# Which half's norm comes first: the order of root, diagonal, spread and scalings at the start of the second layer

## The chip, the core and the metric

The kernel runs on one core of one Trainium2 chip. The metric is the device time of one execution in microseconds (us). The kernel before takes 1287.84 us, the median of three runs (1287.13, 1287.84 and 1291.49).

## The reference

A backbone of two layers works on 1024 tokens of width 1024. The first layer (a convolution branch and a recurrent branch, with 256 context tokens) ends in a gated residual. The second layer is the one that matters here:

```python
x = x + gate * out_x                       # end of the first layer
hx = rmsnorm(x, norm_g) * (1 + scale) + shift   # the second norm
u, g = split(hx @ w_in, 2)                 # 2048 columns each
d = windowed_mean(u) - u                   # windows 2, 4, 8, 16 within rows of 64 tokens
y = einsum(d, w_grp) * od_scale            # four groups of 512 x 512
x = x + gate * ((y * silu(g)) @ w_out)
return rmsnorm(x, final_g)
```

All of it is float32. The root of the norm is one number per token: one over the square root of the mean of the squares of its 1024 features.

## The kernel before, in words

**Layout.** Features lie on the partitions, tokens along the free axis: `x1` is eight tiles `x_0` to `x_7` of 128 features by 1024 tokens. The tokens are worked in two halves of 512, called half 0 and half 1 here; `HALF[h]` is the slice of a tile.

**Float32 products.** TensorE multiplies rounded operands, so each operand is split in a high part and a low part (`split`, L101 to L103: a cast on ScalarE, then a subtraction on VectorE or GpSimd). A product is then three matmuls: high by high (L998), high by low (L1000), low by high (L1001). Names that end in h and l are such parts.

**The seven-product scheme.** The large products of the second layer cut both operands in 2 x 2 blocks and form seven block products in place of eight (`quad`, L1009 to L1037). The token operands are b11, t1, t2, b21, t3, b22 and t4, each of four tiles; they are sums and differences of the scaled quarters of `x1`, made in a loop over i (L1354 to L1373). The weights go through `wquad` (L960 to L990), which loads two raw tiles (`wr_`), forms sums (`ws_v` and the like) and splits them (`wq_v`). In `quad`, three PSUM banks are used: qa takes the first product (b11), is copied by ScalarE into bank qb (L1014), qc takes the second (t1), qb the third (t2) on top of the copy, and so on. So the third product can't start before that copy. The products of u (name `v`) and of the gate (name `g`) follow one another in sixteen such groups.

**The fold.** The group weights `w_grp` are multiplied into the columns of `w_in` for u ahead of time, since pooling is linear over tokens (`fold`, L241 to L270). For a group, the raw group weights (`graw`) are loaded and split into gh and gl. Then follow four weight blocks kp: each loads a raw block (`wr_wu`) from SyncE's queue, ScalarE casts it to `wh_wu` (L102), GpSimd makes `wl_wu` (L103), and for two slices s TensorE does twelve matmuls; ScalarE copies the result from PSUM (`fo`, L265) and issues the store to `wfold` in DRAM from its own queue (L266). The tiles of `fo` come from a pool of two, and so do the raw tiles `wr`, which `wquad` uses too. `v_weights` loads the folded weights (`wr_v`) back from `wfold`. Groups 2 and 3 are folded here, between the first layer's last product (`woa`) and the second layer's first one: this is the work that TensorE has while the norm is made.

**The second norm.** While the last products of the first layer come out, `square_acc` adds up the squares of each half in `nacc[h]` (in the profile n1acc). For each half, `rstd_cols` (L196 to L212) does four steps: four matmuls (L202) that sum over the partitions and leave the sums of 512 tokens as four columns; a square root on ScalarE (L203) and a reciprocal on VectorE (L206); a product with the unit matrix on VectorE that makes four diagonal blocks (L208, `dg_n`); and a matmul of ones by these diagonals (L211), which spreads each token's root over all 128 partitions into a PSUM bank (`ms_n`). `scaled` (L1337 to L1340) multiplies a half of a tile by the feature's scale `a` and this spread root: sixteen scalings, 128 by 512 each. Half 1 of the squares is complete first; half 0 gets its last term from the last tile, `x_7`.

**The order.** Each engine works its instructions in one fixed sequence. A scheduler writes it, with its own timeline estimate, from the program order, the dependences and some hints: `high_priority` draws an instruction forward (the copies of `quad` have it, L1013 and following), and `issue_after(x)` keeps the instructions of a block behind x on their engine. In the kernel before, `rstd_cols` is called for half 0 and then for half 1 (L1303); four steps of the two folds are free of it (L1304 and L1305), the rest of the folds stands behind both square roots (L1306 to L1311). In the blocks' loop the scalings of half 0 and half 1 are written by turns.

Of the kernel before, what the change touches and what calls it, by code (L numbers as in the profile page):

```python
# [15 lines left out]
P = 128  # L16
# [39 lines left out]
def body(ctx, tc, xT, ctxT, cc, ccol, modT, modW, win, gw, wout, wu, grp, wg, wo1, small, edge, ident, outT):  # L56
# [136 lines left out]
        nc.vector.reciprocal(acc, rt[:, :n])  # L193


    def rstd_cols(acc, name, idD, rpool, wn, marks=None):  # L196
        n = acc.shape[-1]
        nt = n // P
        ps, root = banks(f"ms_{name}", wn)
        r = rpool.tile([P, H // P], F32, tag=f"rc_{name}", name=f"rc_{name}")[:, :nt]  # L200
        for c in range(nt):
            nc.tensor.matmul(ps[:, c : c + 1], acc[:, c * P : (c + 1) * P], ones[:, 0:1], start=True, stop=True)  # L202
        root_done = nc.scalar.activation(r, ps[:, :nt], AF.Sqrt, bias=eps_r)  # L203
        if marks is not None:
            marks.append(root_done)
        nc.vector.reciprocal(r, r)  # L206
        t = ttile(f"dg_{name}")[:, :n]
        nc.vector.tensor_tensor(out=t.rearrange("p (c t) -> p c t", t=P),  # L208
                                in0=idD.unsqueeze(1).to_broadcast([P, nt, P]),
                                in1=r.unsqueeze(2).to_broadcast([P, nt, P]), op=mult)  # L210
        nc.tensor.matmul(root[:, :n], ones, t, start=True, stop=True)  # L211
        return root[:, :n]  # L212

# [25 lines left out]
    def fold(g, raw_tile, out_tile, g_tile=None, w_tile=None):  # L239
        g_tile = g_tile or dtile  # L240
        gh, gl = [], []  # L241
        for i in range(2):
            raw = raw_tile(f"graw_{g}_{i}")
            load(raw, grp[g, i])
            th = g_tile(f"gh_{g}_{i}", F32R)
            tl = g_tile(f"gl_{g}_{i}", F32R)
            split(raw, th, tl, nc.vector)
            gh += [th[:, 0:H], th[:, H:D]]
            gl += [tl[:, 0:H], tl[:, H:D]]
        yield  # L250
        if w_tile is not None:
            ws = [wload(wu[g, kp], f"wu_{g}_{kp}", nc.gpsimd, out=w_tile[kp]) for kp in range(KT // 2)]
            yield
        for kp in range(KT // 2):
            wh, wl = wload(wu[g, kp], f"wu_{g}_{kp}", nc.gpsimd) if w_tile is None else ws[kp]
            for s in range(2):
                ps = psum(f"fold_{g}_{kp}_{s}")
                for i in range(4):
                    kc = slice(i * 2 * P + s * P, i * 2 * P + (s + 1) * P)
                    nc.tensor.matmul(ps, wh[:, kc], gh[i], start=(i == 0), stop=False)  # L260
                    nc.tensor.matmul(ps, wh[:, kc], gl[i], start=False, stop=False)
                    nc.tensor.matmul(ps, wl[:, kc], gh[i], start=False, stop=(i == 3))
                dst = wfold[g][:, :, 2 * kp : 2 * kp + 2, :]
                o = out_tile(f"fo_{g}_{kp}_{s}")
                nc.scalar.copy(o, ps)  # L265
                nc.scalar.dma_start(dst[:, :, s, :].rearrange("m p c -> p m c"),  # L266
                                    o.rearrange("p (m c) -> p m c", c=P))
            yield
# [1645 lines left out]
```

## Time and profile before

| what | value |
|---|---|
| median of three runs | 1287.84 us (1287.13 to 1291.49) |
| the profiled execution | 1293.0 us |
| its span in the profile | 1291.2 us |
| mean granted clock of TensorE | 0.996 |
| busy: ScalarE, GpSimd | 642.1 us, 353.6 us |
| time of the DMA queues' packets, first queue | 40.3% of 16 engines |
| HBM read and written | 136.72 MB and 44.04 MB |

PE is TensorE's matmuls, PEld its weight loads, DVE is VectorE, ACT ScalarE, POOL GpSimd, SP SyncE; ACTq and SPq are an engine's DMA issues. A row of a timeline gives the start in us from the start of the span, the time in us, the engine, the line of the kernel, the operation, its tiles (out <- in, buffer numbers left out), partitions by elements, and a count where like instructions are drawn together; in square brackets stands the idle time of the engine before it and what ended that. A matmul's row holds its latency: matmuls overlap, so the pitch is the distance of two starts. A table by windows gives, for each stretch, the busy time of PE, PEld, DVE, ACT and POOL in this order (instructions in brackets), then the granted clock (1 is full speed), the busy share of the DMA engines and GB/s.

### The profile page before, as it was taken

The page shows a single profiled execution, that of the slowest core. Times are in us where ns is not written, and L with a number is a line of the kernel's source. Part 1 is how long each engine was busy: PE and PEld are TensorE (multiplying, and loading weights), DVE is VectorE, ACT ScalarE, POOL GpSimd, SP SyncE. Part 2 cuts the span into 40 slices and gives each one's busy share as a digit, 9 for nine tenths or more (in the row PEclk, how much of TensorE's full clock was granted, in tenths as well). Part 3 has the DMA queues.
Part 4 walks back from the last instruction along what each step waited for, and adds up shares of the span by engine and source line. Part 5 has one row for each costly group of instructions (what it writes and reads, how often), then busy time and mean ns, then how long its engine had stood idle before and what let it go on. Part 6 is the DMA issues. An engine that isn't in the chain of part 4 may idle for free.

```text
span 1291.2 us, 15810 instructions
## 1 busy us (share of the span) xinstructions
PE 1272.3 (99%) x5634; PEld 1026.7 (80%) x5634; DVE 1146.3 (89%) x1763; ACT 642.1 (50%) x941; POOL 353.6 (27%) x180
## 2 busy tenths in 40 slices
PE   8999999999999999999999999999999999999997
PEld 4468888888888888888887888788888888878786
DVE  7979999999999989999789758998999987887876
ACT  5343656566657633237435345734434444654543
POOL 3063655675558603543210022000000000000002
PEclk9999999999999999999999999999999999999998
DMA  9934111121212133542555356244233324778723
GB/s 371 355 118 152 58 41 66 41 74 42 66 41 90 55 109 109 182 146 95 171 189 189 129 173 202 83 155 139 93 134 132 123 104 150 246 243 268 285 83 130
DMA packets 82931, 181.80 MB, mean 141 GB/s; under 512 B 7842, under 2 KB 27682, under 8 KB 82852
## 3 DMA queue, kind: packets, MB, share of 16 engines
q1 hardware_dynamic: 74404, 176.60, 40.3%
q10 hardware_dynamic: 8448, 4.20, 1.1%
q8 instruction: 44, 0.72, 0.2%
q14 instruction: 35, 0.29, 0.1%
HBM read 136.72 MB, written 44.04 MB: 140 GB/s over the span
## 4 chain that ended last, share of the span: by engine, by line
PE 82%; DMA 8%; DVE 4%; ACT 2%; issue 2%; POOL 1%; SPq 0%; POOLq 0%; ACTq 0%; DVEq 0%
PE vg L510 7%; PE wob L510 7%; PE va L510 7%; PE gb L510 7%; PE xb L510 6%; PE g L510 4%; PE fold L285 3%; DMA x_part<-xp 2%; PE qb_v L998 2%; PE qb_v L1001 2%; PE qb_v L1000 2%; PE ga L510 2%; PE ga L134 2%; PE ga L133 2%; PE ga L135 2%
## 5 line engine op out<-in xcount | busy, mean ns | idle before, releaser
L510 DVE SCALAR_TENSOR_TENSOR conv<-u,sm,conv 128x505 f32<-128x505 f32 (+6 forms) x224 | 153.7, 744 | 0.9
L1703 POOL TENSOR_TENSOR o<-x,rr 128x256 f32<-128x256 f32 (+1 forms) x10 | 9.4, 970 | 447.6 <-ACT rr L1639 445.7
L510 POOL TENSOR_TENSOR l<-l,l 128x1280 f32<-128x1280 f32 (+1 forms) x23 | 63.9, 2796 | 91.8 <-DVE l L510 65.5
L510 ACT ACTIVATE l<-g,sm 128x512 f32<-128x512 f32 (+1 forms) x96 | 58.7, 619 | 57.8 <-PE g L510 56.0
L285 PE MATMUL fold<-graw,wu 128*128 128x512 f32 x128 | 58.0, 614 | 2.2 <-DMA wu<-wu 2.2
L285 PEld LDWEIGHTS fold<-graw,wu 128*128 128x128 f32 x128 | 25.1, 197 | 33.7 <-issue 32.6
L102 ACT CAST wq_g<-wr_g 128x512 fp32r<-128x512 f32 x48 | 28.3, 621 | 45.6 <-DVE wr_g L979 17.6
L510 PE MATMUL wob<-ybh,wh_wob 128*128 128x512 f32 x128 | 50.6, 396 | 0.0
L510 PE MATMUL gb<-h0h,wl_gb 128*128 128x512 f32 x128 | 49.9, 390 | 0.3 <-POOL wl_gb L510 0.3
L510 PE MATMUL vg<-h0h,wl_vg 128*128 128x512 f32 x128 | 50.0, 390 | 0.0
L510 PE MATMUL gb<-h0h,wh_gb 128*128 128x512 f32 x128 | 49.8, 389 | 0.0
L510 PE MATMUL wob<-ybh,wl_wob 128*128 128x512 f32 x128 | 49.8, 389 | 0.0
L510 PE MATMUL gb<-h0l,wh_gb 128*128 128x512 f32 x128 | 49.8, 389 | 0.0
L510 PE MATMUL vg<-h0h,wh_vg 128*128 128x512 f32 x128 | 49.8, 389 | 0.0
L510 PE MATMUL vg<-h0l,wh_vg 128*128 128x512 f32 x128 | 49.8, 389 | 0.0
L510 PE MATMUL va<-h0h,wh_va 128*128 128x512 f32 x128 | 49.8, 389 | 0.0
L510 PE MATMUL va<-h0l,wh_va 128*128 128x512 f32 x128 | 49.8, 389 | 0.0
L510 PE MATMUL va<-h0h,wl_va 128*128 128x512 f32 x128 | 49.8, 389 | 0.0
L510 PE MATMUL wob<-ybl,wh_wob 128*128 128x512 f32 x128 | 49.8, 389 | 0.0
L510 DVE TENSOR_TENSOR_SCAN l<-l,l 128x256 f32<-128x256 f32 (+1 forms) x32 | 48.7, 1521 | 1.1
L103 POOL TENSOR_TENSOR wl_wu<-wr_wu,wh_wu 128x1024 fp32r<-128x1024 f32 x8 | 19.2, 2402 | 108.7 <-ACT wh_wu L102 108.7
L510 POOL TENSOR_TENSOR l<-l,uc 128x1280 f32<-128x1280 f32 x16 | 48.2, 3033 | 0.0
(618 smaller groups left out, 4342.9 us busy)
## 6 DMA issues: line engine op xcount, KB each, us to landing
mod<-modT SPq DMA_DIRECT2D x20, 512.0 KB, 5.4
x_part<-xp SPq DMA_DIRECT2D x32, 256.0 KB, 3.5
mod<-modT SPq DMA_DIRECT2D x32, 256.0 KB, 3.3
wr_v<-wfold SPq DMA_DIRECT2D x16, 512.0 KB, 3.4
wr_g<-wg SPq DMA_DIRECT2D x16, 512.0 KB, 4.5
wr_wo<-wo SPq DMA_DIRECT2D x16, 512.0 KB, 4.8
y_b<-y SPq DMA_DIRECT2D x24, 256.0 KB, 3.3
y_t<-y SPq DMA_DIRECT2D x24, 256.0 KB, 3.4
```

What stands on the lines that cost most here:

```text
L102: return (nc.scalar.copy(hi, src), eng.tensor_tensor(out=lo, in0=src, in1=hi.bitcast(F32), op=sub))
L103: eng.tensor_tensor(out=lo, in0=src, in1=hi.bitcast(F32), op=sub))
L133: nc.tensor.matmul(ps, hi[:, kc], xh[k][:, cols], start=(k == 0), stop=False)
L134: nc.tensor.matmul(ps, hi[:, kc], xl[k][:, cols], start=False, stop=False)
L135: nc.tensor.matmul(ps, lo[:, kc], xh[k][:, cols], start=False, stop=(k == ks - 1))
L285: nc.tensor.matmul(ps, w[:, kc], gs[i], start=(i == 0), stop=(i == 3))
L510: last[eng] = f(*args, **kw)
L998: nc.tensor.matmul(ps, hi, xh[k], start=(first and k == 0), stop=False, skip_group_check=not first)
L1000: nc.tensor.matmul(ps, hi, xl[k], start=False, stop=False, skip_group_check=not first)
L1001: mm = nc.tensor.matmul(ps, lo, xh[k], start=False, stop=(k == KH - 1), skip_group_check=not first)
L1703: nc.gpsimd.tensor_tensor(out=outs[k // per][:, k % per], in0=x1[k][:, cols], in1=rr, op=mult)
```

## The change

`rstd_cols` gives its last column matmul, its diagonal and its spread matmul back in a list, and is called for half 1 first. All of half 0's steps are kept behind half 1's diagonal on VectorE and behind half 1's spread on TensorE. Two pieces of the fold of group 2 are kept behind half 1's steps on TensorE: its second weight block behind the columns, its third behind the spread. The first step of group 3 (loading and splitting its group weights) is kept behind half 1's square root. In the loop over the blocks, the scalings of half 1 other than those of the first i are kept behind half 0's diagonal on VectorE; before that they may come, while half 0's root is still being made.

```diff
-    def rstd_cols(acc, name, idD, rpool, wn, marks=None):
+    def rstd_cols(acc, name, idD, rpool, wn, marks=None, spread=None):
...
         for c in range(nt):
-            nc.tensor.matmul(ps[:, c : c + 1], acc[:, c * P : (c + 1) * P], ones[:, 0:1], start=True, stop=True)
+            col = nc.tensor.matmul(ps[:, c : c + 1], acc[:, c * P : (c + 1) * P], ones[:, 0:1], start=True, stop=True)
...
-        nc.tensor.matmul(root[:, :n], ones, t, start=True, stop=True)
+        mm = nc.tensor.matmul(root[:, :n], ones, t, start=True, stop=True)
+        if spread is not None:
+            spread += [col, diag, mm]
         return root[:, :n]
+
+    pe_order = {}
...
                 ps = psum(f"fold_{g}_{kp}_{s}")
...
+                with ExitStack() as fctx:
+                    for mm in pe_order.get((g, kp, s), ()):
+                        fctx.enter_context(tc.issue_after(mm.ins))
...
     marks = []
-    rs = [rstd_cols(nacc[h][:, :H], f"n1{h}", idD, hpool, h, marks) for h in range(2)]
-    for f in (fold2, fold2, fold3, fold2):
+    spread = []
+    rs = [rstd_cols(nacc[1][:, :H], "n11", idD, hpool, 1, marks, spread)]
+    with tc.issue_after(spread[1].ins), tc.issue_after(spread[2].ins):
+        rs.insert(0, rstd_cols(nacc[0][:, :H], "n10", idD, hpool, 0, marks, spread))
+    pe_order[2, 1, 0], pe_order[2, 2, 0] = spread[:1], spread[2:3]
+    for f in (fold2, fold2):
         next(f)
+    with tc.issue_after(marks[0].ins):
+        next(fold3)
+    next(fold2)
...
         b11, b21 = x1[i][:, HALF[0]], scaled(0, KH + i)
-        b12, b22 = scaled(1, i), scaled(1, KH + i)
+        with ExitStack() as sctx:
+            if i > 0:
+                sctx.enter_context(tc.issue_after(spread[4].ins))
+            b12, b22 = scaled(1, i), scaled(1, KH + i)
```

The first place is VectorE at the norm. In the names, gl are the low parts of group 3's group weights, rc_n the reciprocals, dg_n the diagonals and ms_n the spread roots. Before, dg_n_6063 and ms_n_1 belong to half 0, dg_n_6074 and ms_n to half 1:

```order
L103 TENSOR_TENSOR gl_0_6116<-graw_0_6113,gh_0_6115 128x1024
L206 RECIPROCAL rc_n_6067<-rc_n_6067 128x4
L1275 TENSOR_TENSOR n1acc_5498<-n1acc_5498,n1q_1_0_6049 128x512
L103 TENSOR_TENSOR gl_1_6122<-graw_1_6119,gh_1_6121 128x1024
L206 RECIPROCAL rc_n_6056<-rc_n_6056 128x4
L208 TENSOR_TENSOR dg_n_6063<-cH,rc_n_6056 128x512
L208 TENSOR_TENSOR dg_n_6074<-cH,rc_n_6067 128x512
L1339 SCALAR_TENSOR_TENSOR x_0_5502<-x_0_5502,a_135,ms_n_1_6055 128x512
L1339 SCALAR_TENSOR_TENSOR x_1_5503<-x_1_5503,a_135,ms_n_1_6055 128x512
```

With the change, dg_n_6062 and ms_n_6054 belong to half 1, and dg_n_6074 to half 0:

```order
L206 RECIPROCAL rc_n_6055<-rc_n_6055 128x4
L208 TENSOR_TENSOR dg_n_6062<-cH,rc_n_6055 128x512
L103 TENSOR_TENSOR gl_0_6116<-graw_0_6113,gh_0_6115 128x1024
L1282 TENSOR_TENSOR n1acc_5498<-n1acc_5498,n1q_1_0_6049 128x512
L103 TENSOR_TENSOR gl_1_6122<-graw_1_6119,gh_1_6121 128x1024
L1353 SCALAR_TENSOR_TENSOR x_0_5502<-x_0_5502,a_135,ms_n_6054 128x512
L1353 SCALAR_TENSOR_TENSOR x_4_5790<-x_4_5790,a_135,ms_n_6054 128x512
L206 RECIPROCAL rc_n_6067<-rc_n_6067 128x4
L208 TENSOR_TENSOR dg_n_6074<-cH,rc_n_6067 128x512
L1353 SCALAR_TENSOR_TENSOR x_1_5503<-x_1_5503,a_135,ms_n_6054 128x512
L1353 SCALAR_TENSOR_TENSOR x_5_5791<-x_5_5791,a_135,ms_n_6054 128x512
```

Half 1's diagonal has moved ahead of both low splits of the fold, and its scalings begin ahead of half 0's reciprocal; before, both diagonals stood behind the splits, with no scaling between.

The second place is ScalarE at the first group of `v`: the high splits of the token operands (x_b22h, x_t2h, x_b21h, with the tile of `x1` that they come from), a copy of the fold (fo), the copy of `quad` from bank qa to bank qb, and the copy of a finished bank (s_v). Before:

```order
L1334 ACTIVATE x_b21h_6409<-x_5_5791,m_134 128x512
L266 DMA wfold_84<-fo_3_1_6402 128x4x128
L1014 COPY qb_v_6569<-qa_v_6567 128x512
L1334 ACTIVATE x_b22h_6426<-x_6_5936,m_134 128x512
L1334 ACTIVATE x_b22h_6426<-x_7_5937,m_134 128x512
L1334 ACTIVATE x_t2h_6414<-x_3_5645,m_134 128x512
L1334 ACTIVATE x_b21h_6410<-x_6_5936,m_134 128x512
L1334 ACTIVATE x_b21h_6410<-x_7_5937,m_134 128x512
L1042 COPY s_v_6595<-qc_v_6568 128x512
```

With the change:

```order
L1348 ACTIVATE x_b22h_6425<-x_5_5791,m_134 128x512
L273 DMA wfold_84<-fo_3_0_6386 128x4x128
L272 COPY fo_3_1_6402<-fold_3_1_6389 128x512
L1348 ACTIVATE x_b22h_6426<-x_6_5936,m_134 128x512
L1348 ACTIVATE x_b22h_6426<-x_7_5937,m_134 128x512
L1348 ACTIVATE x_t2h_6414<-x_3_5645,m_134 128x512
L1348 ACTIVATE x_b21h_6410<-x_6_5936,m_134 128x512
L1348 ACTIVATE x_b21h_6410<-x_7_5937,m_134 128x512
L1021 COPY qb_v_6569<-qa_v_6567 128x512
L273 DMA wfold_84<-fo_3_1_6402 128x4x128
L1049 COPY s_v_6595<-qc_v_6568 128x512
```

The copy from qa to qb stood ahead of five splits and stands behind them now, and one fold copy with its store has moved into the stretch.

The third place is TensorE at the same group, where the second product (qc_v, token operand t1) meets the third (qb_v, token operand t2). Before:

```order
L998 MATMUL qc_v_6568<-x_t1h_6418,wq_v_5_6456 128x512
L998 MATMUL qb_v_6569<-x_t2h_6413,wq_v_6_6459 128x512
L1000 MATMUL qb_v_6569<-x_t2l_6415,wq_v_6_6459 128x512
L1001 MATMUL qb_v_6569<-x_t2h_6413,wq_v_6_6459 128x512
L998 MATMUL qb_v_6569<-x_t2h_6413,wq_v_6_6459 128x512
L1000 MATMUL qb_v_6569<-x_t2l_6415,wq_v_6_6459 128x512
L1000 MATMUL qc_v_6568<-x_t1l_6420,wq_v_5_6456 128x512
L1001 MATMUL qc_v_6568<-x_t1h_6418,wq_v_5_6456 128x512
```

With the change:

```order
L1005 MATMUL qc_v_6568<-x_t1h_6418,wq_v_5_6456 128x512
L1007 MATMUL qc_v_6568<-x_t1l_6420,wq_v_5_6456 128x512
L1008 MATMUL qc_v_6568<-x_t1h_6418,wq_v_5_6456 128x512
L1005 MATMUL qb_v_6569<-x_t2h_6413,wq_v_6_6459 128x512
L1007 MATMUL qb_v_6569<-x_t2l_6415,wq_v_6_6459 128x512
L1008 MATMUL qb_v_6569<-x_t2h_6413,wq_v_6_6459 128x512
L1005 MATMUL qb_v_6569<-x_t2h_6413,wq_v_6_6459 128x512
L1007 MATMUL qb_v_6569<-x_t2l_6415,wq_v_6_6459 128x512
```

The last two matmuls of the second product now stand ahead of the third product, where five matmuls of it stood before them.

More of the change, by code (lines that the diff above doesn't have):

```diff
@@ L257, in fold @@
                 ps = psum(f"fold_{g}_{kp}_{s}")
[L258 to L262, printed above, removed]
+                with ExitStack() as fctx:
+                    for mm in pe_order.get((g, kp, s), ()):
+                        fctx.enter_context(tc.issue_after(mm.ins))
+                    for i in range(4):
+                        kc = slice(i * 2 * P + s * P, i * 2 * P + (s + 1) * P)
+                        nc.tensor.matmul(ps, wh[:, kc], gh[i], start=(i == 0), stop=False)
+                        nc.tensor.matmul(ps, wh[:, kc], gl[i], start=False, stop=False)
+                        nc.tensor.matmul(ps, wl[:, kc], gh[i], start=False, stop=(i == 3))
                 dst = wfold[g][:, :, 2 * kp : 2 * kp + 2, :]
```

6 lines of the change are left out of this document (3 added, 3 removed).

## The prediction

> **What bounds the kernel now.** I read the page first, then the PE waits, then the timelines of the engines backwards from the longest wait. The page's first line:
>
> ```profile
> PE 1272.3 (99%) x5634; PEld 1026.7 (80%) x5634; DVE 1146.3 (89%) x1763; ACT 642.1 (50%) x941; POOL 353.6 (27%) x180
> ```
>
> PE is the bound: a microsecond counts only where PE waits for it. The waits of PE from 700 us to the end, the two largest (total, times, longest):
>
> ```profile
> PE qb_v L998 <- ACT qb_v L1014: 2.1, 1, 2.1
> PE qb_wo L998 <- ACT b_wo L1563: 1.3, 2, 0.7
> ```
>
> The first lies right behind the changed stretch. PE around it, from the timeline:
>
> ```profile
> 816.44 0.39 PE L1001 MATMUL qc_v<-x_t1h,wq_v 128*128 128x512 f32 x1
> 816.66 0.39 PE L998 MATMUL qc_v<-x_t1h,wq_v 128*128 128x512 f32 x1
> 819.19 0.67 PE L998 MATMUL qb_v<-x_t2h,wq_v 128*128 128x512 f32 x1 [2.14 <-ACT qb_v L1014]
> ...
> 822.64 0.45 PE L998 MATMUL qb_v<-x_t2h,wq_v 128*128 128x512 f32 x1
> 822.93 0.39 PE L1000 MATMUL qb_v<-x_t2l,wq_v 128*128 128x512 f32 x1
> ```
>
> and the table by windows (busy times, then the granted clock, DMA share, GB/s):
>
> ```profile
> 815.00:820.00 5.00, 2.86 (x12) 2.06 (x11) 5.00 (x9) 5.00 (x10) 0.09 (x2) 0.94 0.19 54
> 820.00:825.00 5.00, 5.00 (x18) 3.92 (x16) 5.00 (x9) 2.83 (x5) 0.24 (x2) 0.72 0.61 201
> ```
>
> PE stands still for 2.14 us, and then its clock is granted at half: 0.94 and 0.72 over 5 us each are 0.3 + 1.4 = 1.7 us lost in about 3.4 us. So this place costs about 3.8 us. In those two windows DVE is busy for 5.00 of 5.00 us, and in the first ACT too: the wait is for a copy that stands in ACT's queue behind the splitting of operands, and the splits come from DVE. ACT's timeline (ACTq rows are its DMA issues):
>
> ```profile
> 783.61 1.05 ACT L102 CAST wh_wu<-wr_wu 128x1024 fp32r<-128x1024 f32 x1 [1.54 <-DMA wr_wu<-wu]
> 783.62 0.98 ACTq L266 DMA_DIRECT2D wfold<-fo  x2
> 788.35 0.59 ACT L265 COPY fo<-fold 128x512 f32<-128x512 f32 x1 [3.69 <-DMA wfold<-fo]
> ...
> 790.46 1.05 ACT L102 CAST wh_wu<-wr_wu 128x1024 fp32r<-128x1024 f32 x1 [0.44 <-ACT fo L265]
> ...
> 793.23 2.56 ACT L1334 ACTIVATE x_b11h<-x,m 128x512 fp32r<-128x512 f32 x4
> ...
> 809.89 0.72 ACT L1334 ACTIVATE x_t2h<-x,m 128x512 fp32r<-128x512 f32 x1 [0.44 <-DVE x L1361]
> 810.52 0.57 ACT L265 COPY fo<-fold 128x512 f32<-128x512 f32 x1
> ...
> 818.55 0.58 ACT L1014 COPY qb_v<-qa_v 128x512 f32<-128x512 f32 x1
> ...
> 820.92 1.33 ACT L1334 ACTIVATE x_b21h<-x,m 128x512 fp32r<-128x512 f32 x2
> ```
>
> The copy that PE waits for starts at 818.55. From 809.89 on ACT does not wait; at 809.89 it waited for DVE. DVE's timeline:
>
> ```profile
> 777.89 1.23 DVE L103 TENSOR_TENSOR gl<-graw,gh 128x1024 fp32r<-128x1024 f32 x1 [1.46 <-ACT gh L102]
> 779.03 0.17 DVE L206 RECIPROCAL rc_n<-rc_n 128x4 f32<-128x4 f32 x1
> 779.24 1.29 DVE L208 TENSOR_TENSOR dg_n<-cH,rc_n 128x512 f32<-128x512 f32 x2
> 784.00 10.62 DVE L1339 SCALAR_TENSOR_TENSOR x<-x,a,ms_n 128x512 f32<-128x512 f32 x16 [3.48 <-PE ms_n L211]
> 794.54 4.36 DVE L1335 SCALAR_TENSOR_TENSOR x_b11l<-x,m,x_b11h 128x512 fp32r<-128x512 f32 x4
> 798.83 0.68 DVE L103 TENSOR_TENSOR wq_v<-wr_v,wq_v 128x512 fp32r<-128x512 f32 x1
> 799.75 0.69 DVE L978 TENSOR_TENSOR ws_v<-wr_v,wr_v 128x512 f32<-128x512 f32 x1 [0.25 <-DMA wr_v<-wfold]
> ...
> 808.93 1.28 DVE L1361 TENSOR_TENSOR x<-x,x 128x512 f32<-128x512 f32 x2
> ...
> 818.39 0.68 DVE L103 TENSOR_TENSOR x_t1l<-x,x_t1h 128x512 fp32r<-128x512 f32 x1
> ```
>
> The 3.48 us before the 16 scalings is the idle time that the change goes for: the larger part of this stall looks like its child. But at 799.75 DVE waits once more, 0.25 us, for a weight load that has nothing to do with the norm. That load on the chain that ended last, and POOL's last work before it:
>
> ```profile
> 796.39 3.33 DMA wr_v<-wfold
> ```
>
> ```profile
> 791.59 4.78 POOL L103 TENSOR_TENSOR wl_wu<-wr_wu,wh_wu 128x1024 fp32r<-128x1024 f32 x2 [4.44 <-ACT wh_wu L102]
> ```
>
> The load takes the buffer that POOL's second split leaves at 796.37, and lands at 799.72.
>
> **The change part by part.** *Half 1 first.* Its reciprocal and diagonal come before the next fold's low split; DVE is idle there, and ACT's square root falls in a wait for a load. Nothing on the path; if that cover were gone, 0.17 + 0.65 us of DVE. The spread of half 1 on PE moves forward by one fold block; PE's work is the same. What it costs PE, from the timeline:
>
> ```profile
> 784.96 1.02 PE L211 MATMUL ms_n<-dg_n,ones 128*128 128x512 f32 x2
> ```
>
> So all behind it up to its old place, the columns of half 0 and its spread among them, comes under 1.02 us later on PE (I take 0.9), and what follows is at its old time: 0 in the sum.
>
> *The scalings.* DVE in the new order, by the pitch 10.62 / 16 = 0.66 us: the low split ends at 779.12; two scalings of half 1, to 780.45; reciprocal and diagonal of half 0, 0.17 + 0.65, to 781.3; six scalings, 4.0, to 785.2; by then the spread of half 0 has been through PE (its old release, 784.00, and 0.9); eight scalings, 5.3, to 790.5. Before, the 16 ended at 794.6. DVE gains 4.1 us here: the part does what it says.
>
> *What is late next.* Behind the scalings stand the four low splits x_b11l, which need the casts x_b11h on ACT. These stood at 793.23 without having waited for DVE: ahead of them ACT had to cast the fold's last weights, behind fold copies that waited 3.69 us for stores. The change leaves that queue as it is, and puts one store issue and one more fold copy ahead of the casts: they start 1 us later, near 794.3. So DVE, free at 790.5, idles to about 794.9. The first low split takes long anyway:
>
> ```profile
> L1335 DVE SCALAR_TENSOR_TENSOR x_b11l<-x,m,x_b11h x4: 741/742/2372, 794.5 to 798.2; 128x512 fp32r<-128x512 f32 x4
> ```
>
> 2.37 us against 0.74: it ends half a microsecond after POOL's split (796.37), and will again. DVE then arrives at ws_v as before, at 799.5, and waits for the load to 799.75. Its order from there to the second copy of t1 is unchanged, and it is busy all the time. Of the 4.1 us nothing is left at 799.75. Is the load itself earlier? It hangs on POOL, POOL on the cast at 790.46, that on the fold stores issued at 783.62, those on the load before 783.61, and that on the low split at 777.89, which waits for ACT, not for the norm. None of these is moved. I take 0; bounds of 1 us to both sides, for stores and loads that meet in another order.
>
> *The queue on ACT.* This is the term that remains. From x_t2h at 809.89 on, ACT has the same splits as before, but the copy qb_v<-qa_v now stands behind all of them: behind both x_b22h of blocks 6 and 7, x_t2h of block 3 and both x_b21h of blocks 6 and 7, where it stood ahead of these. One fold copy more (0.57, as at 810.52) falls into this stretch, and the copy itself (0.58) leaves it: they cancel. So the copy starts where the x_b21h at 820.92 end, about 822.15 since neighbours overlap by 0.1, instead of 818.55: +3.6 us. Who waits for it: PE's product qb_v, and everything behind it on PE.
>
> *PE ahead of the copy.* Two matmuls of qc_v, the third block's last two, now stand ahead of qb_v. They need x_t1l, which DVE ends at 819.07, so PE does them inside its wait: at its pitch of 0.22 us (816.44 to 816.66), -0.45 us.
>
> *The clock.* After 2.14 us of idling the half clock took 1.7 us. The new idling is 5.7 us with two matmuls in it. I take 1.7 us again, as the row of the same place; the ends are 0 and 3.4, a second stretch of the same length. The Trainium skill, "TensorE: Matmul & The Clock Gate", section "Part 1: The HAM clock gate", says that the clock is set by windows of 3413 ns which run freely and don't start with the kernel's idling; that fits the 3.4 us here, and by it the slow time after a restart depends on where in a window PE starts again. An estimate from that page: 0 to 6.8 us slow, the sum below from +1.4 to +4.8 us.
>
> *Later order.* The next products are interleaved otherwise (qa_g ahead of the third part of qb_v), SP swaps some stores and loads behind that, none is added. PE's later waits are at most 0.7 us each (second row of the waits): 0, ends -0.7 and +0.7.
>
> Sum: 3.6 - 0.45 + 0 + 0 = +3.15 us, taken as +3.1. Against the profiled execution: 1293.0 (span 1291.2 and 1.8 around it) becomes 1296.1. The profiled execution lies 5.2 us over the median of the three runs, 1287.84, which I take as the base: 1290.9.
>
> **The rivals.**
>
> *The gain arrives.* If the load landed 4 us earlier, or ACT passed its splits to DVE earlier, the copy would stand where PE never waits, and both the 2.1 us and the 1.7 us go: 1287.84 - 3.8 = 1284.0. For it: DVE does gain 4.1 us at 790.5. Against: the wait at 799.75 and POOL's row, neither of which the change touches. It decides when the load lands before 796. Chance 0.10.
>
> *A part arrives.* One of the fold's stores goes out earlier than I think, and the load lands 1 to 3 us earlier; each microsecond takes as much off the copy's start. At 2 us: 1288.9. Chance 0.13.
>
> *The clock's second stretch.* The longer idling covers the whole of one stretch of 3.4 us, so PE starts again at half clock and keeps it for a second one: 1.7 us more, +4.8, 1292.6. That is slower by more than the 0.3% (3.9 us) which a measurement of this kernel can tell from no change. For it: 2.1 us of idling already took the clock. Against: the two matmuls in the idling, and that the row shows only one stretch. It decides from an idling that outlasts the stretch after the drop; the Trainium skill's windows, above, allow it. Chance 0.17.
>
> **How the numbers follow.** The forecast has 0.60: predicted 1290.9, its own range 1289.5 to 1292.3 by the load's bound of 1 us and the later order's 0.7. The range of 8 in 10 takes in most of the part that arrives and the second stretch, and leaves out the full gain and the tails: 1287.0 to 1293.2. Faster by over 0.3% (under 1283.98): half of the full gain and little else, 0.06. Slower by over 0.3% (over 1291.70): the second stretch, 0.15 of it, and a quarter of the forecast's own 0.60, less a little: 0.28. Within: 0.66.
>
> **What would show it.** Right: in the profile after, the 16 scalings end near 790.5; DVE idles some 4 us before x_b11l and stands at ws_v at about 799.75; the copy qb_v<-qa_v starts near 822; PE's waits there are about 2 and 3 us with two matmuls between. Wrong: if ws_v comes before 798, the load was not the gate; if the copy starts before 819, ACT's queue is not full where I think; if the copy is late and PE does not wait, another product fills the gap.

## The result, and the profile after

The changed kernel takes 1294.47 us, the median of 22 runs (1290.88 to 1297.96); the kernel before, in 22 runs, 1290.36 us (1287.13 to 1295.96). The ratio is 1.0031, with a 95% interval of 1.0021 to 1.0040: 4.0 us slower, 2.7 to 5.2. The forecast of the change was +3.1 us; the forecast of the time, 1290.9 with a range up to 1293.2, is 3.6 us too low. These two misses have different causes, and the second is the larger.

In the profiled execution (1293.88 us, span 1292.1) nearly every step stands where the prediction put it. PE's two largest waits behind 600 us:

```profile
PE qb_v L1005 <- ACT qb_v L1021: 2.6, 1, 2.6
PE qc_v L1007 <- DVE x_t1l L103: 1.8, 1, 1.8
```

VectorE's timeline:

```profile
779.48 1.40 DVE L1353 SCALAR_TENSOR_TENSOR x<-x,a,ms_n 128x512 f32<-128x512 f32 x2
780.79 0.17 DVE L206 RECIPROCAL rc_n<-rc_n 128x4 f32<-128x4 f32 x1
781.00 0.69 DVE L208 TENSOR_TENSOR dg_n<-cH,rc_n 128x512 f32<-128x512 f32 x1
781.61 9.30 DVE L1353 SCALAR_TENSOR_TENSOR x<-x,a,ms_n 128x512 f32<-128x512 f32 x14
793.90 4.27 DVE L1349 SCALAR_TENSOR_TENSOR x_b11l<-x,m,x_b11h 128x512 fp32r<-128x512 f32 x4 [2.99 <-ACT x_b11h L1348]
...
799.73 0.69 DVE L985 TENSOR_TENSOR ws_v<-wr_v,wr_v 128x512 f32<-128x512 f32 x1 [0.95 <-DMA wr_v<-wfold]
```

The scalings end at 790.9 (790.5 was forecast, 794.6 before): the part does what it says. Then VectorE idles 2.99 us for the casts on ScalarE and 0.95 us for the load, and stands at ws_v at 799.73, where it stood at 799.75 before. The chain that ended last runs through just this link:

```profile
790.88 4.77 POOL wl_wu L103 x2
795.67 4.04 DMA wr_v<-wfold
799.73 0.70 DVE ws_v L985
```

ScalarE's timeline at the copy, and PE's:

```profile
819.85 0.72 ACT L1348 ACTIVATE x_t2h<-x,m 128x512 fp32r<-128x512 f32 x1
820.47 1.33 ACT L1348 ACTIVATE x_b21h<-x,m 128x512 fp32r<-128x512 f32 x2
821.69 0.59 ACT L1021 COPY qb_v<-qa_v 128x512 f32<-128x512 f32 x1
```

```profile
818.96 0.50 PE L1007 MATMUL qc_v<-x_t1l,wq_v 128*128 128x512 f32 x1 [1.75 <-DVE x_t1l L103]
819.29 0.40 PE L1008 MATMUL qc_v<-x_t1h,wq_v 128*128 128x512 f32 x1
822.33 0.80 PE L1005 MATMUL qb_v<-x_t2h,wq_v 128*128 128x512 f32 x1 [2.64 <-ACT qb_v L1021]
...
826.34 0.47 PE L1005 MATMUL qb_v<-x_t2h,wq_v 128*128 128x512 f32 x1
```

The copy starts 3.14 us later than before, and so does PE's third product (822.33 for 819.19). The forecast had 3.6 us for both; the 0.45 us of the two matmuls that move ahead comes off behind the third product. The clock, too, is another than the sum has it. The table by windows:

```profile
815.00:820.00 5.00, 2.94 (x12) 1.80 (x10) 5.00 (x9) 5.00 (x10) 0.47 (x4) 0.96 0.26 73
820.00:825.00 5.00, 2.67 (x6) 2.16 (x7) 5.00 (x9) 2.79 (x5) 0.00 (x0) 0.50 0.84 301
825.00:830.00 5.00, 5.00 (x20) 4.01 (x19) 5.00 (x9) 2.93 (x5) 0.00 (x0) 0.85 0.12 48
```

Granted clocks of 0.96, 0.50 and 0.85 are about 0.4, 5.0 and 1.5 us at half speed (the shares are rounded), 6.8 us in all, twice the 3.4 us of the profile before. 2.7 us of it fall in the idling (from 819.6 to 822.3); in the other 4.1 us PE works at half speed and loses 2.1 us.

To compare stretches I use two matmuls of PE: the last one of the first layer's product, and the first one of the third group of v. Before, then after:

```profile
768.78 0.39 PE L1001 MATMUL qb_woa<-ya_t4h,wq_woa 128*128 128x512 f32 x1
...
889.37 0.39 PE L998 MATMUL qa_v<-x_b11h,wq_v 128*128 128x512 f32 x1
```

```profile
768.79 0.39 PE L1008 MATMUL qb_woa<-ya_t4h,wq_woa 128*128 128x512 f32 x1
...
892.42 0.39 PE L1005 MATMUL qa_v<-x_b11h,wq_v 128*128 128x512 f32 x1
```

120.6 us became 123.6 us: +3.0, as the sum has it. Against its own profiled execution the forecast is right to 0.1 us, and that is partly luck: the copy's delay came out 0.5 us under its term, and the half clock took 0.4 us more than in the profile before (2.1 for 1.7), where the sum has no difference. So the experiments have two questions: whether the loss has the cause that was forecast, and what the kernel before usually does at this place.

### The profile page after: what moved, and what is told of

The parts are those of the page before. It is cut to its first block, busy times and chain, and to the rows that moved or that the text cites. A ratio compares the mean times of both kernels' runs of the same rounds, so it can differ in the third digit from the quotient of the medians.

```text
span 1292.1 us, 15806 instructions
## 1 busy us (share of the span) xinstructions
PE 1272.0 (98%) x5634; PEld 1027.3 (80%) x5634; DVE 1142.7 (88%) x1763; ACT 641.0 (50%) x941; POOL 353.6 (27%) x180
## 4 chain that ended last, share of the span: by engine, by line
PE 85%; DMA 5%; DVE 4%; ACT 3%; issue 2%; POOL 1%; SPq 0%; POOLq 0%; DVEq 0%; ACTq 0%
PE vg L517 7%; PE gb L517 7%; PE wob L517 7%; PE va L517 7%; PE xb L517 6%; PE g L517 4%; PE fold L292 3%; PE qb_v L1005 2%; PE qb_v L1008 2%; PE qb_v L1007 2%; PE ga L517 2%; PE qb_g L1008 2%; PE qb_g L1005 2%; PE qb_g L1007 2%; PE ga L134 2%; PE ga L133 2%
```

## The experiments

Ratios are to the kernel before on the same chip; us are worked out with 1290.4.

### Is it the copy's place on ScalarE?

**Without the rule on the scalings.** The edit takes back one of the parts; half 1 still comes first:

```diff
-        with ExitStack() as sctx:
-            if i > 0:
-                sctx.enter_context(tc.issue_after(spread[4].ins))
-            b12, b22 = scaled(1, i), scaled(1, KH + i)
+        b12, b22 = scaled(1, i), scaled(1, KH + i)
```

> The changed kernel without the one rule in the blocks' loop that keeps the scalings of half 1 behind half 0's diagonal; half 1 still comes first, and the fold's blocks stay where the change put them. On ScalarE the copy from qa to qb stands ahead of the last five splits again, as before the change. Queue theory (the loss is the copy's place on ScalarE): the copy starts near 818.5, PE waits for it about 2.1 us, and the time is that of the kernel before, within 0.7 us. Rival (the loss comes from the norm's new order or from the fold's blocks on TensorE, which this kernel keeps): 3 to 4 us over the kernel before.

Measured: ratio 0.9990 (0.9980 to 1.0001), -1.3 us (-2.6 to +0.1). The loss is gone; the rival, which would have kept 3 to 4 us, is out. Its ScalarE at the copy, its wait of PE and its VectorE at ws_v:

```profile
816.30 0.58 ACT L1021 COPY qb_v<-qa_v 128x512 f32<-128x512 f32 x1
816.81 1.34 ACT L1348 ACTIVATE x_b22h<-x,m 128x512 fp32r<-128x512 f32 x2
```

```profile
PE qb_v L1005 <- ACT qb_v L1021: 1.0, 1, 1.0
```

```profile
797.01 0.68 DVE L985 TENSOR_TENSOR ws_v<-wr_v,wr_v 128x512 f32<-128x512 f32 x1
```

The copy stands ahead of the five splits again, and the two matmuls of the second product behind the start of the third, so this run takes back both reorderings at once. PE waits 1.0 us, not the 2.1 us that I expected. In this execution VectorE was 2.7 us earlier at ws_v. That was the first sign that this place is not the same in every execution.

**The copy put first.** Five splits are written behind the copy, in `quad`, and kept there. The same edit with nine splits makes the two kernels after it:

```diff
             evac = nc.scalar.copy(b, a)
+        if behind is not None:
+            with tc.issue_after(evac.ins):
+                behind()
...
+    late = {"t2": (3,), "b21": (2, 3), "b22": (2, 3)}
```

> The changed kernel, with five splits (x_t2h of block 3, x_b22h and x_b21h of blocks 6 and 7) kept behind the copy from qa to qb on ScalarE. Queue theory: the copy starts near 818.7 in place of 821.7, PE starts the third product near 819.5 in place of 822.3, so about 2.8 us less than the changed kernel, near the kernel before (0 to +1 us). Rival (VectorE or the later order sets the time, not the copy): PE waits as long for a low split behind the copy, and the time stays 3 to 4 us over the kernel before.

Measured: ratio 1.0014 (1.0003 to 1.0026), +1.8 us (+0.4 to +3.4). Its copy starts at 817.91, and PE has one wait left here:

```profile
818.25 0.50 PE L1007 MATMUL qc_v<-x_t1l,wq_v 128*128 128x512 f32 x1 [1.93 <-DVE x_t1l L103]
```

So about 2 us of the 4 go with the copy's place; the interval is wide. What is left is a wait for VectorE, since the two matmuls that the new order puts ahead of the third product need x_t1l and hold it back too, and a half clock of 3.4 us behind that wait (granted 0.96 and 0.70 in the windows 815:820 and 820:825).

**The copy put early, in both kernels.** The nine splits are x_t2h of block 3, and all of b21 and b22.

> The changed kernel, with nine splits (x_t2h of block 3 and all of x_b21h and x_b22h) kept behind the copy. Queue theory: the copy starts near 816.5, right after PE would ask for it, and PE keeps working on the third product; the wait of 2.6 us and the half clock behind it go, 5 to 7 us under the changed kernel, 2 to 3.5 us under the kernel before. Rival (VectorE, busy all the time here, is the next bound): PE waits for the low splits x_t1l and x_b21l in place of the copy, 1.5 to 2.5 us in all, and the time is within 1 us of the kernel before.

> The kernel before, with the same nine splits kept behind the copy. Queue theory: the copy starts near 816.1, PE starts the third product at once, and the wait of 2.14 us goes; with waits of about 1.3 us for x_b21l in its place, too short to take the clock, 2 to 3.5 us under the kernel before. Rival (VectorE is the bound behind the copy): as long a wait for x_b21l and a half clock again, within 0.7 us of the kernel before. If the norm's early scaling is worth anything where the copy is early, the other kernel of this kind (the changed one) is 0.5 to 1 us faster than this one; by the forecast's account (the gain is lost at the load of the folded weights) the two are equal within 0.5 us.

Measured: the changed kernel with the early copy has 0.9991 (0.9981 to 1.0001), -1.2 us; the kernel before with it 1.0005 (0.9994 to 1.0016), +0.6 us. In the changed kernel the loss of 4 us is gone. This edit takes the wait for x_t1l and the half clock away together with the wait for the copy (granted 1.00 from 815 to 830), so it doesn't price the copy's place alone. And neither is 2 us faster than the kernel before. In the first PE waits at most 0.25 us:

```profile
820.10 0.50 PE L1007 MATMUL qb_v<-x_t2l,wq_v 128*128 128x512 f32 x1 [0.25 <-DVE x_t2l L1352]
```

In the second two new waits stand in the old one's place, both for VectorE:

```profile
PE qc_g L1001 <- DVE wq_g L103: 1.0, 1, 1.0
PE qa_v L1000 <- DVE x_b21l L1338: 0.9, 1, 0.9
```

The rival has it there, in the waits and in the time; the half clock that it expected too did not come. The two ratios differ by 0.0014, with intervals that overlap: what the early scalings are worth where the copy is early is not settled.

### What does the half clock cost?

**The waits filled with matmuls.** The results of these matmuls are read by nobody (`spare` is a PSUM bank that is free here); the edit touches nothing that PE waits for, but the scheduler writes the order behind it anew. In the changed kernel 7 and 11, in the kernel before 9:

```diff
+                    for _ in range(warm[0]):
+                        with tc.issue_after(mm.ins):
+                            mm = nc.tensor.matmul(spare, p5[:, 0:P], th[0], start=True, stop=True)
...
+                for _ in range(warm[1]):
+                    with tc.issue_after(last.ins):
+                        last = nc.tensor.matmul(spare, p5[:, 0:P], ops["t1"][0][0], start=True, stop=True)
```

> The changed kernel, with matmuls whose result nobody reads in PE's two waits at the first group of v: 7 in the wait for x_t1l, 11 in the wait for the copy, 0.22 us each, 4.0 us in 4.4 us of idling. What PE waits for stays as it is; only its clock has no reason to fall. Clock theory (of the loss of about 4 us, some 2 us are the half clock behind the longer idling, 4.15 us of work at half speed in the profile): the granted clock stays 1.0 there, and the time is 1.5 to 2.1 us under the changed kernel, about 2.2 us over the kernel before. Rival (the clock costs the changed kernel no more than the kernel before, and the rest of the loss is elsewhere): within 0.5 us of the changed kernel, 3.5 to 4.5 us over the kernel before.

> The kernel before, with 9 such matmuls (2.0 us) in its wait of 2.14 us for the copy. Clock theory, as it has to be for the changed kernel to lose 4 us: in most executions of the kernel before the wait of 2.14 us doesn't take the clock, and its profiled execution, which lost 1.7 us so, was not typical: this kernel is within 0.6 us of the kernel before. Rival (the profiled execution was typical): 1.4 to 1.7 us under the kernel before.

Measured: the changed kernel filled, 1.0027 (1.0015 to 1.0038), +3.5 us (+1.9 to +4.9); the kernel before filled, 1.0002 (0.9992 to 1.0012), +0.3 us (-1.0 to +1.5). In the first the clock stays up:

```profile
820.00:825.00 5.00, 4.66 (x19) 3.56 (x20) 5.00 (x9) 4.06 (x7) 0.24 (x2) 1.00 0.66 204
825.00:830.00 5.00, 5.00 (x24) 4.12 (x23) 5.00 (x9) 2.54 (x5) 0.24 (x2) 1.00 0.40 163
```

and yet its stretch between the two matmuls is 122.9 us, 0.7 less than 123.6, not 2.1 less. But this is not the changed kernel at full clock. Behind the filling the scheduler has put the product with t4 ahead of qc_g and qb_g, and there PE waits; in the changed kernel that product comes later and waits for nothing. The kernel with the filling, then the changed one:

```profile
838.23 0.50 PE L1005 MATMUL qb_v<-x_t4h,wq_v 128*128 128x512 f32 x1 [0.72 <-ACT vp L1537]
```

```profile
843.91 0.39 PE L1005 MATMUL qb_v<-x_t4h,wq_v 128*128 128x512 f32 x1
```

The time, 0.5 us less than the changed kernel with intervals of over 1 us on both, is the rival's. Since the order changed with the clock, it doesn't say what the clock costs the changed kernel; that can be read from repeated profiles, below, and there it is the full price. In the kernel before, the filling brings nothing. But nine matmuls are as long as the wait of its first profile, and where the wait is shorter they hold PE up themselves: in this execution the copy ended at 817.60, and the third product started at 819.18. So that the 1.7 us of the first profile is unusual is shown only by the repetitions.

### Is the load the gate for VectorE?

**The fold's last low part on VectorE.** GpSimd made the last two one after the other, and the load takes the buffer that the second one leaves.

```diff
-            ws = [wload(wu[g, kp], f"wu_{g}_{kp}", nc.gpsimd, out=w_tile[kp]) for kp in range(KT // 2)]
+            ws = [wload(wu[g, kp], f"wu_{g}_{kp}", nc.vector if (g, kp) in ((3, 3),) else nc.gpsimd, out=w_tile[kp])
+                  for kp in range(KT // 2)]
```

> The changed kernel, with the low part of the fold's very last weight block (group 3, kp 3) made by VectorE, which idles there, and not by GpSimd behind its block before. Load theory (the gain of the early scalings is lost because the load of the folded weights waits for the buffer that GpSimd's last split leaves): that buffer is free at 794.0 in place of 795.6, ws_v starts at 798.2 in place of 799.7, the copy 1.5 us earlier, 1.3 to 1.6 us under the changed kernel, about 2.7 us over the kernel before. Rival (the fold's stores or ScalarE's casts hold VectorE anyway): ws_v within 0.4 us of 799.7 and the time within 0.5 us of the changed kernel.

Measured: ratio 1.0028 (1.0017 to 1.0040), +3.6 us: that of the changed kernel, as the rival has it. But its profile has ws_v at 796.39, 3.3 us earlier, and a stretch of 120.3 us. It was therefore profiled twice more, unchanged:

> The changed kernel with the fold's last low split on VectorE, profiled again. If the release of the buffer holds the load: ws_v 13.5 to 14.2 us ahead of the first product of v (12.2 in the changed kernel), PE's waits 2.6 to 3 us in all. If other transfers hold it: ws_v 12 to 12.5 us ahead, waits of 4.4 us as in the changed kernel, and the first profile was the exception.

> The same kernel once more: as for its first repetition, 13.5 to 14.2 us ahead and 2.6 to 3 us of waits, or 12 to 12.5 us ahead and 4.4 us of waits.

One of the two (1292.08 us) is as the first, with ws_v at 797.10; the other (1295.42 us) is as the changed kernel. VectorE's timeline there:

```profile
762.86 2.69 DVE L1283 TENSOR_TENSOR n1acc<-n1acc,n1q 128x512 f32<-128x512 f32 x1 [4.33 <-ACT n1q L1282]
...
794.52 1.23 DVE L103 TENSOR_TENSOR wl_wu<-wr_wu,wh_wu 128x1024 fp32r<-128x1024 f32 x1 [2.31 <-ACT wh_wu L102]
...
799.91 0.69 DVE L986 TENSOR_TENSOR ws_v<-wr_v,wr_v 128x512 f32<-128x512 f32 x1 [0.91 <-DMA wr_v<-wfold]
```

Here the split was taken from GpSimd and the load is no earlier, since the split itself waits 2.31 us for ScalarE's cast of the fold's weights. The two early executions don't prove the moved split's worth either: in both of them the add of the first row took 0.69 us, and so it did in the kernel before with the filled wait, where GpSimd makes the split and the load is as early (ws_v 14.1 us ahead of the first product of v, as in these two with 14.2 and 14.1). So the release by GpSimd is the last link, and moving it alone brought nothing in that execution and nothing in the median; the links ahead of it differ from execution to execution. The first profile, at 1290.01 us, was the fastest of its kernel's 12 runs (up to 1297.17), not a typical one.

**Without the rule, and with the copy early.**

> The changed kernel without the rule on the scalings, as in the first experiment, and with the nine splits kept behind the copy. There VectorE is already 2.7 us earlier and PE waits 1.0 us for the copy. Queue theory: that wait goes, and no new one over 0.5 us comes: 0.7 to 1.2 us under the first experiment, 2 to 2.4 us under the kernel before. Rival (VectorE is the next bound, x_b21l above all): a wait of about 1 us for a low split in its place, the time of the first experiment within 0.4 us.

Measured: ratio 1.0004 (0.9992 to 1.0017), +0.5 us. Expected were 2 us under the kernel before; the rival, the time of the first experiment, is nearer. Its profile has ws_v at 801.90, and PE waits 0.5 us for x_t2h and 0.4 us for x_b22l.

### Why do executions differ?

The rows of VectorE's add of a square at the end of the first layer (n1acc) tell two groups apart. In the first profile of before, then in the kernel before with the filled wait, whose order at this place is the same:

```profile
761.79 2.52 DVE L1275 TENSOR_TENSOR n1acc<-n1acc,n1q 128x512 f32<-128x512 f32 x1 [4.71 <-ACT n1q L1274]
```

```profile
761.49 0.69 DVE L1298 TENSOR_TENSOR n1acc<-n1acc,n1q 128x512 f32<-128x512 f32 x1 [4.22 <-ACT n1q L1297]
```

In the first the add starts 0.4 us behind the start of GpSimd's second low part (about 761.4), and is held; in the second it starts 0.4 us ahead of it (761.87), and is not. The Trainium skill, "SBUF — State Buffer", section "Who interferes with whom", says that a VectorE instruction with two inputs in SBUF and a GpSimd instruction that reads SBUF block each other for a whole instruction, whichever starts first; 2.52 us beside 0.69 us agree. In the sixteen profiles without the swap below, the four with this add at 0.69 us have ws_v between 796.4 and 797.4, the twelve with a held add between 799.0 and 801.9. That the add is the cause is argued, not shown: behind it stand the residual of x, the stores of x on SyncE, and behind these the fold's next loads.

**One swap on ScalarE**, so that the add never meets the second split, in three kernels:

```diff
+                with ExitStack() as qctx:
+                    if (g, kp) == (2, 1):
+                        qctx.enter_context(tc.issue_after(squares[-4].ins))
+                    ws.append(wload(wu[g, kp], f"wu_{g}_{kp}", nc.gpsimd, out=w_tile[kp]))
```

> The kernel before with one swap on ScalarE and nothing else in another order: at the end of the first layer the square of a block of x_6 goes ahead of the cast wh_wu of the fold's second weight block (group 2, kp 1). Theory of two patterns: in some executions VectorE's add of that square (n1acc, near 761.8) starts just behind GpSimd's second split of the fold and is held for 2.5 us, in others it comes just ahead and takes 0.7 us; the held add delays SyncE's stores of x, the fold's loads behind them, and in the end the load of v's weights by 2.5 us. With the swap the add always comes first: 0.7 us, ws_v at 797.0 to 797.6, the copy about 1.1 us earlier against PE than in the profile of before, PE's wait 1.0 us with the clock kept; 0.8 to 2 us under the kernel before, since part of its executions are of this pattern anyway. Rival (the add's hold is a symptom and the load's time is set by other transfers): ws_v stays near 799.7, the time within 0.6 us of the kernel before.

> The changed kernel with the same one swap. Theory of two patterns: ws_v near 797.3 in place of 799.7, the copy some 2 us earlier than 821.7, PE's waits 2.2 to 2.6 us in all in place of 4.4: 1.5 to 2.5 us under the changed kernel, still 1.5 to 3 us over the kernel before with this swap, since the copy stands behind the same five splits. Rival: ws_v near 799.7, the time of the changed kernel within 0.6 us.

> The changed kernel without the rule on the scalings (the first experiment) with the same swap; the profile of the first experiment was of the early pattern. Theory of two patterns: this kernel's profile is as that one, PE's wait for the copy about 1.0 us, and its times scatter less; 0.5 to 1 us under the first experiment's 1289.5, about 2 us under the kernel before, and equal to the kernel before with the swap within 0.6 us if the new order of the norm is worth nothing of its own. Rival: the first experiment's time within 0.4 us.

Measured: 1.0005 (0.9992 to 1.0018), 1.0036 (1.0021 to 1.0052) and 1.0000 (0.9987 to 1.0014): +0.6, +4.6 and 0.0 us. The times are the rival's: no kernel got faster. In the profiles ws_v lies 14.1, 13.5 and 13.4 us ahead of the first product of v, where it lay 12.2 and 12.3 us ahead in the two first profiles. In the changed kernel that is an earlier load: ws_v stands 29.7 us behind the last matmul of the first layer's product, 30.5 to 30.9 without the swap. In the kernel before it is not: 30.9 us with the swap and 29.9 to 31.0 without, and PE came later to v, behind a wait and a half clock in the fold (last section). The kernel before with the swap:

```profile
759.96 2.53 DVE L1282 TENSOR_TENSOR n1acc<-n1acc,n1q 128x512 f32<-128x512 f32 x1 [2.31 <-ACT n1q L1281]
...
800.10 0.68 DVE L983 TENSOR_TENSOR ws_v<-wr_v,wr_v 128x512 f32<-128x512 f32 x1
```

The add now meets the first split, 2 us earlier, and is held there, in all three kernels. So the swap did not make the add short, as its theory had it, and doesn't test what a short add is worth. PE waits 1.02 us for the copy. In the changed kernel with the swap the two waits are 0.57 and 2.65 us, 3.2 us in place of 4.4, and its stretch is 122.1 us; that this is not seen in its time (8 runs, and an interval of 4 us) stays open. The profile of the kernel before with the swap is that of the slowest of its 12 runs.

**Both kernels profiled again, unchanged.**

> The kernel before, unchanged, profiled again. If its first profile was the rarer pattern: PE's wait for the copy 1.0 us, no half clock there, ws_v 2 to 3 us earlier. If the first was typical: 2.1 us and a half clock of 3.4 us again.

> The changed kernel, unchanged, profiled again. With the load of v's weights at the earlier time: waits of 2.5 to 3.2 us in all, with one half clock stretch or none; at the later time, as in its first profile: 4.4 us and a half clock.

> The kernel before, unchanged, profiled once more: as for the first repetition, wait of 1.0 us and full clock, or 2.1 us and half clock.

> The changed kernel, unchanged, profiled once more: as for its first repetition, 2.5 to 3.2 us of waits, or 4.4 us.

The times were 1290.92 and 1290.19 us for the kernel before, 1296.86 and 1296.73 us for the changed one. The first repetition of before, at the copy, in its windows and at the ends of the stretch:

```profile
819.04 0.50 PE L998 MATMUL qb_v<-x_t2h,wq_v 128*128 128x512 f32 x1 [1.02 <-ACT qb_v L1014]
```

```profile
815.00:820.00 5.00, 3.98 (x18) 3.00 (x17) 5.00 (x9) 5.00 (x10) 0.23 (x2) 1.00 0.18 54
820.00:825.00 5.00, 5.00 (x23) 3.84 (x22) 5.00 (x9) 2.56 (x5) 0.24 (x2) 1.00 0.62 210
```

```profile
769.69 0.39 PE L1001 MATMUL qb_woa<-ya_t4h,wq_woa 128*128 128x512 f32 x1
...
887.99 0.39 PE L998 MATMUL qa_v<-x_b11h,wq_v 128*128 128x512 f32 x1
```

and the first repetition of after, its waits and its stretch:

```profile
PE qb_v L1005 <- ACT qb_v L1021: 2.6, 1, 2.6
PE qc_v L1007 <- DVE x_t1l L103: 1.9, 1, 1.9
```

```profile
768.97 0.39 PE L1008 MATMUL qb_woa<-ya_t4h,wq_woa 128*128 128x512 f32 x1
...
892.55 0.39 PE L1005 MATMUL qa_v<-x_b11h,wq_v 128*128 128x512 f32 x1
```

The last two columns of the table give the part of the half clock that falls behind the restart with the third product, where PE works, and the time from that product to the third group of v.

| profiled execution | stretch | waits of PE at the copy | at half clock | behind the restart | third product to third group |
|---|---|---|---|---|---|
| before, first | 120.6 us | 2.14 us | 3.4 us | 3.4 us | 70.2 us |
| before, repeated | 118.3 and 118.2 us | 1.02 and 1.14 us | none | none | 68.9 and 69.1 us |
| after, first | 123.6 us | 1.75 + 2.64 us | 6.8 us | 4.1 us | 70.1 us |
| after, repeated | 123.6 and 123.6 us | 1.89 + 2.64 and 2.11 + 2.63 us | 6.8 us in each | 5.1 and 4.4 us | 70.5 and 70.2 us |

In two profiles of three the kernel before waits 1.0 to 1.1 us and keeps its clock, and these two (1290.92 and 1290.19 us) lie near its median of 22 runs, the first (1293.0) does not; so I take the first for the rarer case. What differs is not the load: ws_v, expected 2 to 3 us earlier, stands at 799.78 and 799.70, and the add was held (2.71 and 2.57 us). PE comes 0.9 us later to this place (769.69 for 768.78), while the copy is ready at about the same time. The changed kernel is the same in all three. Its third product starts 3.0 and 3.1 us later than that of before in the repetitions (822.03 and 821.92 for 819.04 and 818.82), as in the first pair. The third group of v begins at 888.0 and 887.9 in the repetitions of before, at 892.55 and 892.1 in those of after: 4.4 us, beside the measured 4.0.

The table also gives the price of the half clock. With half of the time behind the restart taken off, the three profiles of after come to about 68.0 us each, and the kernel with the split on VectorE, whose order behind the restart differs only in the place of eight matmuls, took 68.15 us in its first repetition, at full clock throughout. So the changed kernel pays 2.1 to 2.6 us for it, half of the time in full, and no later wait takes that up.

## Why the prediction was wrong, step by step

- **Half 1 first, the scalings.** As forecast: they end at 790.9, a gain of 3.7 us on VectorE.
- **What is late next.** As forecast: VectorE idles 2.99 us for x_b11h and 0.95 us for the load, and ws_v stands at 799.73. The prediction follows the load back from GpSimd to ScalarE's cast and further into the fold; with the last split moved to VectorE that split waited for the same cast, and the load came no earlier. Shown is that the gain is lost at the load and at x_b11h; which link of the fold sets the load stays open.
- **The queue on ScalarE.** As forecast in kind, and shown by experiment: with the rule on the scalings taken out, or with the copy put early, the loss is gone. The term of 3.6 us came out as 3.14 in the first profile and about 3.05 in the repetitions. It is that rule which let ScalarE's order change, not the order of the two halves.
- **The clock.** "I take 1.7 us again" is the step of the forecast of the change that failed: it set 1.7 us after against 1.7 us before, and so nothing in the sum. The kernel before lost nothing to the clock here in two profiles of three; the changed kernel has the second stretch, the rival to which I gave 0.17, in three of three, and loses 2.1 to 2.6 us.
- **The kernel before as it was profiled.** It is this term that hangs on the first profile, not the wait of 2.14 us, which stands in no term of the sum. The terms as the repetitions have them: about +3.05 for the copy, -0.45 for the two matmuls, and +1.8 in the place of 0, which is what is left of the 4.4 us at the third group. The sum of +3.1 is too small by 0.9 against the measured 4.0 (2.7 to 5.2).
- **The base.** "The median of the three runs, 1287.84, which I take as the base" is the step that put the time outside the range. In 22 runs the base is 1290.36, 2.5 us higher. The ratio on the old base gives 1291.8, inside the range. Two of the three runs are the lowest and the third lowest of the 22. The three themselves lay 4.4 us apart, and the profiled execution 5.2 us above their median; the range had no term for it. It was also inconsistent: the base came from the lowest executions, the stall from a high one.
- **The gain or a part of it arrives.** Neither happened in the changed kernel.

What stays open: how often each group of executions occurs, what sets the load in each, and why the kernels whose load came earlier in their profiles (the swap in the changed kernel, the split on VectorE) show none of it in their medians. A part of the answer may be scatter: from the third group of v to the end of the span, the three profiles of the one changed kernel took 399.7, 402.5 and 402.8 us. Of the kernels tried none is faster than the kernel before by more than the measurement can tell; the nearest are the one without the rule (0.9990) and the changed one with an early copy (0.9991).

## What to carry to other kernels

When an engine gains time, follow it to its next wait that has nothing to do with the gain, and then look at what the scheduler did with the order of the other engines: here the gain ended at a load, and a reordered queue on ScalarE, with the half clock behind the longer wait, cost 4 us. One profile shows one execution; a wait of 2 us with a half clock behind it may be the rare case, so profile the kernel before twice before you price a stall. An edit that is to test one cost can make the scheduler write another order behind it, so compare the orders before you read the time. A range round a median of three runs needs a term for the median itself.

## What the runs showed of the hardware

- A VectorE add of two 128x512 tiles took 0.69 us alone and 2.45 to 2.76 us when GpSimd's split ran at its start.
- At this place the half clock came only in lengths of 3.4 and 6.8 us; in the first profile of after it began at about 819.6, as PE stopped, and lasted on through 4.1 us of work. A wait of 1.0 to 1.1 us did not take it in any of five profiles at this place; waits of 2.14 and 1.93 us did. In the kernel before with the swap it fell once behind a wait of 0.95 us and 1.05 us of the norm's narrow column matmuls, in the fold:

```profile
770.52 1.05 PE L202 MATMUL ms_n<-ones,n1acc 128*128 128x1 f32 x8 [0.95 <-DVE n1acc L1282]
...
772.32 0.63 PE L267 MATMUL fold<-gh,wl_wu 128*128 128x512 f32 x1
```

- The same wait can take the clock in one execution and not in another. The changed kernel with the split on VectorE, in its first profile and in the first repetition:

```profile
818.98 0.80 PE L1006 MATMUL qb_v<-x_t2h,wq_v 128*128 128x512 f32 x1 [2.63 <-ACT qb_v L1022]
```

```profile
819.70 0.50 PE L1006 MATMUL qb_v<-x_t2h,wq_v 128*128 128x512 f32 x1 [2.63 <-ACT qb_v L1022]
```

  The first restarts at half clock (0.80 us for a matmul) and has a stretch of 120.3 us, the second at full clock, with 119.2 us. Their first matmuls of the third group of v:

```profile
888.68 0.39 PE L1006 MATMUL qa_v<-x_b11h,wq_v 128*128 128x512 f32 x1
```

```profile
887.85 0.39 PE L1006 MATMUL qa_v<-x_b11h,wq_v 128*128 128x512 f32 x1
```

  From the restart that is 69.70 us and 68.15 us: 1.55 us for 3.3 us of work at half clock. In the changed kernel with the swap PE restarted behind 2.65 us at full clock (0.50 us) and was at half clock (0.63 us) 1.5 us later.
- The Trainium skill, "TensorE: Matmul & The Clock Gate", section "Why this matters for your kernels", warns of PE gaps of over some 3 us between matmuls. Here 1.93 and 2.14 us were enough; the measurement decides.
